# Four pairs by seven products in the down projections and in gate and up, with half tiles and plain banks added by transfers

## The chip, the cores and the metric

The kernel runs on one core of a Trainium2 chip. The metric is the device time of one execution in microseconds (us). A core has five engines that run side by side, each through its own instructions in order: TensorE (PE in the profile; its weight loads are PEld), VectorE (DVE), ScalarE (ACT), GpSimd (POOL) and SyncE (SP). Here SP and POOL only start transfers, apart from a few copies on POOL in the linear attention. TensorE writes its results to eight PSUM banks; VectorE and ScalarE take them out to the on-chip memory, SBUF.

## The reference

One residual block on x (256 frames by 2048), all in float32:

```
x = x + 1/2 * SwiGLU_1(RMSNorm(x))          SwiGLU(h) = (silu(h @ w_gate) * (h @ w_up)) @ w_down
h = RMSNorm(x);  P = h @ W_in               all projections of the mixing part
m = sigmoid(gate_gdn) * (gated_deltanet(P) @ W_A) + sigmoid(gate_att) * (chunk_attention(P) @ W_B)
x = x + m @ W_out
x = x + 1/2 * SwiGLU_2(RMSNorm(x))
```

w_gate and w_up are 2048 by 5504, w_down is 5504 by 2048. The change lies in the two SwiGLU blocks (the FFNs). A k tile below is 128 rows of a weight, of the dimension that is summed over.

## The kernel before, in words

**Products.** For accuracy every float32 operand is split into a high part, rounded to the matmul's format (a ScalarE cast, `L364`, `L395`, `L397`, `L121`), and the rest (a VectorE subtraction, `L418`, `L122`). A product of two blocks is then three matmuls: high by high, high by low, low by high (`product`, L440; `L446` to `L448`). Activations stand still in the array, 128 columns at a time, and weights stream through, 512 columns to a matmul.

**Pairs.** Work goes in pairs: two k tiles, two weights (gate and up, or two column blocks of down) and both halves of the 256 frames. That is a 2 by 2 block product of 8 products, 24 matmuls: a plain pair. Its weights cost one cast and one subtraction of 128x2048. A pair by seven products (Winograd's form of Strassen's method) has 7 products, 21 matmuls. Its weights cost more: VectorE first forms four sums (`L390` to `L392`, tile `s`), then the parts that are used as they are (`w`, `v`) and the sums are split (`L395`, `L397`, three runs of `L418`). Its activations need sums too (`act_sums`, L136).

**seven** (L473) runs eight pairs into PSUM. Plain pairs add into banks 2, 3, 4 and 8, and pairs by seven products into banks 1 to 7. Which pairs go by products is given by a tuple: `FAST` = (0, 2, 5) in gate and up, `DOWN` = (2, 4, 6) in the down of 16 k tiles and in some projections of the mixing part. After the last pair by products, `L513` to `L517` combine banks 1, 5, 6 and 7 into four SBUF tiles (`wide`, eight buffers); after the last pair `L522` adds the four other banks. Four banks (1 to 4) come from the pool `acc`, four from `core`, which transposes use as well.

**An FFN** (`ffn`, L545) has 43 k tiles of hidden width in 11 tiles of gate and up (ten of 4 k tiles, one of 3), in three chunks, `CHUNKS` = tiles 0 to 3, 4 to 7, 8 to 10. After the gate-and-up tiles of a chunk (`gate_up`, L525) comes the chunk's part of the down projection. In the first two chunks it has 16 k tiles and is two runs of `seven`, each for two of the four column blocks. Its four results are added to the residual in DRAM (`xd`) by transfers that add, started on POOL (`L585`). The third chunk's down has 11 k tiles, all plain. It fetches `xd`, adds, and goes on to the norm or the output. The first tile of the first FFN is plain in all pairs, in the order `FIRST`, since the activations still arrive.

**Hidden blocks.** The output of a gate-and-up tile is transposed on TensorE and split (`hidden`, L549) in two jobs, which run in the next tile, late in its pairs (`jobs` in `seven`), or after some steps of the down. For blocks that meet a pair by products in the down, `hidden` also makes and splits sums (`shid`, `hs`).

**Order and memory.** Weights come in one order, given by `plan` (L268). `load` starts the transfers on SP, `begin` (L346) emits the casts and sums of one item, `prepare` (L410) the subtractions; `take_weights` (L423) keeps over five products' or pieces' worth prepared ahead (`PREP`) and two loads beyond that (`LOAD`). A scheduler then puts the instructions of each engine in an order and hands out buffers. Nearly all large tiles share one pool, the heap: `NB` = 23 slots of 128x2048 float32. A plain pair takes three slots (raw, high, low), a pair by products six (raw, s, w, v, sh, sl), although `v` (`w2` in the code, L379) fills only half of its slot. Raw and s come free after the subtractions, the others after the matmuls. Activations of a norm (class `Xr`, L145 on) take a whole slot for a pair by products and half a slot for a plain one: six slots for (0, 2, 5). A down of 16 k tiles holds four slots of hidden blocks and two of their sums besides.

**Mixing** (linear attention, chunk attention, gates, output projection) lies between the FFNs and uses the same heap. Its tile `kd` (L841) fills half a slot.

Of the kernel before, what the change touches and what calls it, by code (L numbers as in the profile page):

```python
# [17 lines left out]
P = 128  # L18
T = 256
D = 2048  # L20
KD = D // P
# [3 lines left out]
W = H * P  # L25
EPS = 1e-6
BIG = 1e30
NB = 23
FAST = (0, 2, 5)
DOWN = (2, 4, 6)  # L30
FIRST = (1, 3, 4, 6, 7, 0, 2, 5)
QUAD = {2: (0, 0), 3: (1, 0), 4: (0, 1), 8: (1, 1)}
CHUNKS = ((0, 4), (4, 8), (8, 11))
B32 = 32
# [4 lines left out]
def block_kernel(ctx: ExitStack, tc: tile.TileContext, a: dict, out: bass.AP):  # L39
# [14 lines left out]

    def heap(shape, dt, name):
        return hp.tile(shape, dt, tag="h", name=name)

    def acc_bank(name):
        return accp.tile([P, 512], F32, tag="acc", name=name)
# [197 lines left out]
    FG = [(c, min(4, KF - c)) for c in range(0, KF, 4)]  # L257

    def fast_pairs(f, i):
        return () if f == "1" and i == 0 else FAST  # L260

    def pairs_of(f, i):
        return FIRST if f == "1" and i == 0 else range(KD // 2)

    def down_pairs(a0, a1):
        return DOWN if sum(FG[a1 - 1]) - FG[a0][0] == 16 else ()

    def plan():  # L268

        for f in "12":  # L270
            for a0, a1 in CHUNKS:
                for i in range(a0, a1):
                    c, m = FG[i]
                    js = pairs_of(f, i)
                    gu = zip(*(t_pieces(a[w + f], c, m, 0, KD, [2 * j for j in js]) for w in ("wg", "wu")))
                    for j, p in zip(js, gu):
                        yield j in fast_pairs(f, i), p
                k0, k1 = FG[a0][0], sum(FG[a1 - 1])
                cols = lambda d: t_pieces(a["wd" + f], 4 * d, 4, k0, k1)
                if down_pairs(a0, a1):  # L280
                    for d in (0, 2):
                        yield from sevens(cols(d), cols(d + 1))
                else:
                    for d in range(4):
                        yield from twos(cols(d))
            if f == "2":
                return
            yield from mixing()
# [2 lines left out]
        for p in pieces:  # L291
            yield False, (p, next(pieces))

    def sevens(one, two):
        for j, pieces in enumerate(zip(one, two)):
            yield j in DOWN, pieces

    def mixing():
        c0 = 0
# [46 lines left out]
    def begin():  # L346


        while len(loaded) < 1 + LOAD and len(loaded) < left[0]:
            load()  # L350
        left[0] -= 1
        i, fast, pieces, raw = loaded.popleft()
        if not fast:
            out = []
            ms = [n * kk * (P if len(src.shape) == 3 else 1) for src, n, kk in pieces]
            cuts = [(slice(0, 2), ms[0])] if ms[0] == ms[1] else [(slice(at, at + 1), m) for at, m in enumerate(ms)]
            hl = [heap([P, 2, 1024], F32R, f"w{x}{i}") for x in "hl"]
            if i < 3:
                cuts = [(slice(at, at + 1), m) for at, m in enumerate(ms)]
            todo = [tuple(w[:, at, :m] for w in (*hl, raw)) for at, m in cuts]  # L360
            if i == 0:
                todo = [tuple(by_k(w[:, at], k) for w in (*hl, raw)) for at in range(2) for k in range(2)]
            for hi, _, src in todo:
                nc.scalar.copy(hi, src)  # L364
            for at, (src, n, kk) in enumerate(pieces):
                if len(src.shape) == 3:
                    n *= P
                    cols = [w[:, at, : ms[at]].rearrange("p (c k x) -> p c k x", k=kk, x=P) for w in hl]
                    cols = [[w[:, :, j, :] for j in range(kk)] for w in cols]
                else:  # L370
                    cols = [[w[:, at, j * n : (j + 1) * n] for j in range(kk)] for w in hl]
                out.append((1, (*cols, n)))
            begun.append((todo, out))
            return
        tiled = len(pieces[0][0].shape) == 3
        n = pieces[0][1] * (P if tiled else 1)
        s = heap([P, 4, n], F32, f"s{i}")
        w1 = heap([P, 2, 2 * n], F32R, f"w{i}")
        w2 = heap([P, 2, n], F32R, f"v{i}")  # L379

        def by_row(w):

            if tiled:
                return w.rearrange("p b (c k x) -> p b k c x", k=2, x=P)
            return w.rearrange("p b (k n) -> p b k n", k=2)

        col = lambda w: w.rearrange("p (c x) -> p c x", x=P) if tiled else w
        R = by_row(raw[:, :, : 2 * n])
        S = s.rearrange("p b (c x) -> p b c x", x=P) if tiled else s
        nc.vector.tensor_sub(S[:, 0:2], R[:, 1], R[:, :, 0])  # L390
        nc.vector.tensor_add(S[:, 2], S[:, 1], R[:, 0, 0])
        nc.vector.tensor_sub(S[:, 3], R[:, 0, 1], S[:, 2])  # L392
        parts = [(w1[:, 0], w1[:, 1], raw[:, 0, : 2 * n]), (col(w2[:, 0]), col(w2[:, 1]), R[:, 1, 1])]
        for hi, lo, src in parts:
            nc.scalar.copy(hi, src)  # L395
        sh, sl = (heap([P, 4, n], F32R, f"s{x}{i}") for x in "hl")
        nc.scalar.copy(sh, s)  # L397
        parts.append((sh, sl, s))
        k = by_row(w1)
        w11, w21 = ([k[:, s, b] for s in range(2)] for b in range(2))  # L400
        t1, t3, t2, t4 = ((sh[:, b], sl[:, b]) for b in range(4))
        w22 = (w2[:, 0], w2[:, 1])

        prods = ((1, 0, w11), (2, 2, w21), (6, 5, t2), (7, 6, t3), (4, 3, t4), (5, 4, t1), (3, 7, w22))
        begun.append((parts, [(4, prods)]))
# [64 lines left out]
        return tp.tile([P, 512], F32, name=name, tag="w", bufs=8)[:, :n]  # L470


    def seven(nm, n, fast, act, jobs=(), feed=None, pairs=range(KD // 2)):  # L473

        size = {b: len(fast) for b in range(1, 9)}
        for b in (2, 3, 4, 8):
            size[b] += 2 * (KD // 2 - len(fast))
        size[8] -= len(fast)  # L480
        done = dict.fromkeys(size, 0)
        banks = {}

        def add(b, act, wt):
            if b not in banks:
                banks[b] = (acc_bank if b < 5 else core_bank)(f"p{nm}_{b}")[:, :n]
            done[b] += 1
            product(banks[b], act, wt, done[b] == 1, done[b] == size[b])

        ev = {}  # L490
        idle = 0
        for at_pair, j in enumerate(pairs):
            if j in fast:
                ps = take_weights()
                for at, (b, i7, w) in enumerate(ps):
                    add(b, act(j, i7), w)
                    if at == 3:
                        tick()
            else:
                for s in range(2):  # L500
                    wh, wl, _ = take_weights()
                    if feed and s == 0:
                        feed(at_pair)
                    for k, w in enumerate(zip(wh, wl)):
                        for t in range(2):
                            add((2, 4, 3, 8)[2 * s + t], act(j, 2 * k + t), w)
                    idle += 1
                    if idle > 3 and jobs and j > max(fast, default=-1):
                        jobs.popleft()()
            if fast and j == fast[-1]:  # L510
                idle = 1
                g0, u0, g1, u1 = (wide(f"e{nm}_{x}", n) for x in range(4))
                nc.scalar.copy(g0, banks[1])  # L513
                nc.vector.tensor_add(u0, banks[6], g0)
                nc.vector.tensor_add(g1, banks[7], u0)
                nc.vector.tensor_add(u1, banks[5], g1)
                nc.vector.tensor_add(u0, banks[5], u0)  # L517
                ev = {2: g0, 3: u0, 4: g1, 8: u1}
        if not fast:
            return banks  # L520
        for b in (2, 3, 4, 8):
            nc.vector.tensor_add(ev[b], banks[b], ev[b])  # L522
        return ev
# [21 lines left out]
    def ffn(nm, xr, nxt, feed):  # L545
# [15 lines left out]
        for a0, a1 in CHUNKS:  # L561
# [18 lines left out]
            if fast:  # L580
                block = lambda j, b: act(2 * j + b // 2, b % 2) if b < 4 else [sums[j][:, s, b - 4] for s in range(2)]
                for d in (0, 2):
                    ev = seven(f"d{nm}_{a0}{d}", 512, fast, block)
                    for b, (dd, t) in QUAD.items():
                        nc.gpsimd.dma_start(xd[d + dd][t], ev[b], accum_op=ALU.add)  # L585
                continue
            for d in range(4):
                pd = pair(f"pd{nm}_{a0}{d}")
# [244 lines left out]
    def gdn_core(blk, dec, res):  # L833
# [4 lines left out]
        yield 1  # L838

        ss = sp.tile([P, 2, 2, H], F32, name="gdn_ss")  # L840
        kd = heap([P, H, P], F32, "gdn_kd")  # L841
        sqb = heap([P, 4, 4, P], F32, "gdn_sq")
        for i, src in enumerate((KT, QT)):
            for t in range(2):
# [246 lines left out]
                yield 1  # L1091


    xr1 = Xr("1", 0, FAST)

    def stand(k4):

# [19 lines left out]
    def feed(s):  # L1117
# [6 lines left out]
            nc.sync.dma_start(cst, a["cst"])  # L1124
        if s == 6:
            nc.sync.dma_start(hd, a["hd"].partition_broadcast(P))
        if s > 1 and FIRST[s] in FAST:
            xr1.more(FIRST[s], pair_of_x(FIRST[s]))
        for k4 in range(4):
            if s == max(3, *(FIRST.index(2 * k4 + i) for i in range(2))):  # L1130
# [71 lines left out]
            nc.vector.tensor_add(G1[t][:, cs], G1[t][:, cs], s)  # L1202
        after(2, lambda d=d: merged(d))

    xr3 = Xr("3", 2, FAST)
    for d in range(4):
        pss = pair(f"pwo{d}")
        xs = fetch(d, "wo")
# [2 lines left out]
            nc.vector.tensor_add(xs[t], xs[t], pss[t])  # L1211
        norm(xr3, d, xs)

    ffn("3", xr3, None, lambda s: s == 4 and xr3.finish())


# [83 lines left out]
```

## Time and profile before

| What | Value |
|---|---|
| Time, median of 3 runs | 2122.12 us (2122.1 to 2122.61) |
| The profiled execution | 2122.12 us |
| its span in the trace | 2120.4 us |
| granted TensorE clock, mean | 0.999 |
| HBM traffic | 407.72 MB read, 16.79 MB written |
| transfers that add to `xd` (POOL) | 32, 256 KB each |

The profile gives for each engine its busy time, the chain of work that ended last, followed back from the end, and groups of equal instructions with their busy time, their mean duration and the idle time of the engine just before them, with what ended most of it. The two FFNs take 0 to 707.8 us and 1424 to 2120.4 us of the span; the mixing lies between. Matmul records overlap, so the pace of TensorE is read from one start to the next, not from the length of a record.

### The profile page before, as it was taken

The numbers are of one execution on the slowest core, as the hardware profiler recorded it, in microseconds if no ns is written. First come the engines' busy times: TensorE is split into PE (matmuls) and PEld (weight loads), VectorE is DVE, ScalarE is ACT, GpSimd is POOL, SyncE is SP. The second block draws the span as 40 slices with busy tenths as digits, with TensorE's granted clock in tenths as the row PEclk, the third lists the DMA queues.
The fourth block names the chain that finished last, engine by engine and source line by source line (L and its number), as shares of the span: only waits on it lengthen the run. The fifth ranks groups of instructions, "written<-read, shape, count | busy, mean of one in ns | idle before, by whom it ended". The sixth has DMA issues, their size and how long they took to land.

```text
span 2120.4 us, 25501 instructions
## 1 busy us (share of the span) xinstructions
PE 2106.7 (99%) x9804; PEld 1755.5 (83%) x9804; DVE 1704.8 (80%) x1867; ACT 1126.7 (53%) x1125; POOL 36.5 (2%) x45
## 2 busy tenths in 40 slices
PE   9999999999999999999999999999999999999999
PEld 6888888888898988888888888888888888888897
DVE  6888898889976688767785787669888997989782
ACT  6655564545555556567555554456454564545461
POOL 0000000000000000000010000000000100000000
PEclk9999999999999999999999999999999999999999
DMA  9655785558867656536454467666565975569582
GB/s 326 198 186 182 230 250 190 190 164 241 245 196 234 236 179 231 166 120 199 144 179 160 139 200 249 217 197 224 189 195 160 258 231 185 179 180 276 174 275 68
DMA packets 393594, 426.19 MB, mean 201 GB/s; under 512 B 14192, under 2 KB 371840, under 8 KB 393216
## 3 DMA queue, kind: packets, MB, share of 16 engines
q1 hardware_dynamic: 388864, 416.17, 60.6%
q0 software_dynamic: 4608, 8.39, 2.4%
q8 instruction: 77, 1.26, 0.3%
q14 instruction: 45, 0.37, 0.1%
HBM read 407.72 MB, written 16.79 MB: 200 GB/s over the span
## 4 chain that ended last, share of the span: by engine, by line
PE 94%; DVE 3%; ACT 1%; issue 1%; DMA 0%; SPq 0%; DVEq 0%; ACTq 0%
PE pf L447 14%; PE pf L448 14%; PE pf L446 13%; PE pd L447 7%; PE pd L448 7%; PE pd L446 7%; PE pg L447 2%; PE pg L448 2%; PE pg L446 2%; PE pc L446 2%; PE pc L448 2%; PE pc L447 2%; PE pwo L447 1%; PE pwo L446 1%; PE pwo L448 1%; PE hid L131 1%
## 5 line engine op out<-in xcount | busy, mean ns | idle before, releaser
L418 DVE TENSOR_TENSOR wl<-raw,wh 128x2048 fp32r<-128x2048 f32 (+5 forms) x302 | 642.6, 2137 | 68.8 <-ACT wh L364 19.6
L364 ACT CAST wh<-raw 128x2048 fp32r<-128x2048 f32 (+5 forms) x302 | 533.9, 1789 | 130.1 <-PE pd L447 27.3
L446 PE MATMUL pf<-wh,xr 128*128 128x512 f32 (+1 forms) x880 | 337.7, 388 | 3.3 <-ACT xr L173 2.4
L447 PE MATMUL pf<-wl,xr 128*128 128x512 f32 (+1 forms) x880 | 339.3, 386 | 0.2 <-DVE wl L418 0.2
L448 PE MATMUL pf<-wh,xr 128*128 128x512 f32 (+1 forms) x880 | 339.0, 385 | 0.0
L397 ACT CAST sh<-s 128x2048 fp32r<-128x2048 f32 (+1 forms) x99 | 187.0, 1889 | 216.0 <-DVE s L392 204.0
L418 DVE TENSOR_TENSOR sl<-s,sh 128x2048 fp32r<-128x2048 f32 (+1 forms) x99 | 223.5, 2258 | 18.8 <-PE pf L448 6.6
L447 PE MATMUL pd<-wl,hid 128*128 128x512 f32 x496 | 195.4, 394 | 0.0
L446 PEld LDWEIGHTS pf<-wh,xr 128*128 128x128 f32 x880 | 165.4, 188 | 36.1 <-ACT xr L173 2.8
L447 PEld LDWEIGHTS pf<-wl,xr 128*128 128x128 f32 x880 | 165.7, 188 | 33.1 <-DVE wl L418 2.1
L448 PE MATMUL pd<-wh,hid 128*128 128x512 f32 x496 | 193.0, 390 | 0.0
L448 PEld LDWEIGHTS pf<-wh,xr 128*128 128x128 f32 x880 | 165.6, 188 | 31.8 <-DVE xr L174 0.4
L446 PE MATMUL pd<-wh,hid 128*128 128x512 f32 x496 | 185.2, 394 | 0.0
L395 ACT CAST w<-raw 128x1024 fp32r<-128x1024 f32 (+1 forms) x99 | 102.9, 1040 | 119.2 <-PE pd L448 31.3
L390 DVE TENSOR_TENSOR s<-raw 128x1024 f32<-128x1024 f32 (+1 forms) x99 | 119.4, 1206 | 23.6 <-PE pd L447 17.6
L418 DVE TENSOR_TENSOR w<-raw,w 128x1024 fp32r<-128x1024 f32 (+1 forms) x99 | 119.5, 1207 | 6.2 <-ACT w L395 6.0
L447 PEld LDWEIGHTS pd<-wl,hid 128*128 128x128 f32 x496 | 93.2, 188 | 23.5 <-DVE wl L418 5.2
L522 DVE TENSOR_TENSOR ef<-pf,ef 128x512 f32<-128x512 f32 (+1 forms) x84 | 55.5, 675 | 69.2 <-PE pf L448 69.2
L446 PEld LDWEIGHTS pd<-wh,hid 128*128 128x128 f32 x496 | 93.1, 188 | 19.7 <-issue 0.7
L448 PEld LDWEIGHTS pd<-wh,hid 128*128 128x128 f32 x496 | 93.1, 188 | 18.9
L446 PE MATMUL pf<-sh,xf 128*128 128x512 f32 (+1 forms) x252 | 95.9, 386 | 1.7 <-ACT sh L397 1.7
L447 PE MATMUL pf<-sl,xf 128*128 128x512 f32 (+1 forms) x252 | 96.7, 384 | 0.0
(472 smaller groups left out, 3837.0 us busy)
## 6 DMA issues: line engine op xcount, KB each, us to landing
raw<-wd SPq DMA_DIRECT2D x168, 512.0 KB, 5.4
raw<-wg SPq DMA_DIRECT2D x159, 512.0 KB, 3.9
raw<-wu SPq DMA_DIRECT2D x159, 512.0 KB, 5.3
raw<-wgt SPq DMA_DIRECT2D x64, 512.0 KB, 4.5
raw<-wa SPq DMA_DIRECT2D x48, 512.0 KB, 4.6
raw<-wc SPq DMA_DIRECT2D x48, 512.0 KB, 4.7
raw<-wbr SPq DMA_DIRECT2D x32, 512.0 KB, 5.4
raw<-wo SPq DMA_DIRECT2D x32, 512.0 KB, 5.1
```

The lines of the kernel that those rows point to most:

```text
L131: nc.tensor.transpose(ps[:, c * T + t * P : c * T + (t + 1) * P], src(t)[:, (c0 + c) * P : (c0 + c + 1) * P], ident)
L364: nc.scalar.copy(hi, src)
L390: nc.vector.tensor_sub(S[:, 0:2], R[:, 1], R[:, :, 0])
L395: nc.scalar.copy(hi, src)
L397: nc.scalar.copy(sh, s)
L418: nc.vector.tensor_sub(lo, src, f32(hi))
L446: nc.tensor.matmul(dst, ah, wh, start=start, stop=False)
L447: nc.tensor.matmul(dst, ah, wl, start=False, stop=False)
L448: nc.tensor.matmul(dst, al, wh, start=False, stop=stop)
L522: nc.vector.tensor_add(ev[b], banks[b], ev[b])
```

## The change

- Gate and up: the first two tiles of each chunk (but not the plain first tile) have four pairs by products, `FOUR` = (0, 2, 4, 6); the other tiles have (0, 2, 4) in place of (0, 2, 5). `FIRST` and the norm's blocks follow.
- The down of 16 k tiles has four pairs by products, `DEEP` = (2, 3, 5, 6), in place of (2, 4, 6).
- In these downs `L522` is not done. The combined tiles go to `xd` by a transfer that adds, each of the four plain banks is copied by ScalarE to another tile, and that goes to `xd` by a second such transfer.
- `w2` and `kd` move to a pool of two half tiles; the heap has 22 slots in place of 23.
- In `seven`, jobs that are left at the last pair all run after its second half. The norm of the second FFN is finished at the fourth pair in place of the fifth.

```diff
-NB = 23
-FAST = (0, 2, 5)
+NB = 22
+NH = 2
+FAST = (0, 2, 4)
+FOUR = (0, 2, 4, 6)
 DOWN = (2, 4, 6)
-FIRST = (1, 3, 4, 6, 7, 0, 2, 5)
+DEEP = (2, 3, 5, 6)
+FIRST = (1, 3, 5, 7, 0, 2, 4, 6)
...
+    def half_tile(shape, dt, name):
+        return hp.tile(shape, dt, tag="q", name=name, bufs=NH)
...
     def fast_pairs(f, i):
-        return () if f == "1" and i == 0 else FAST
+        if f == "1" and i == 0:
+            return ()
+        return FOUR if any(a0 <= i < a0 + 2 for a0, _ in CHUNKS) else FAST
...
     def down_pairs(a0, a1):
-        return DOWN if sum(FG[a1 - 1]) - FG[a0][0] == 16 else ()
+        return DEEP if sum(FG[a1 - 1]) - FG[a0][0] == 16 else ()
...
-                        yield from sevens(cols(d), cols(d + 1))
+                        yield from sevens(cols(d), cols(d + 1), DEEP)
...
-    def sevens(one, two):
+    def sevens(one, two, fast=DOWN):
         for j, pieces in enumerate(zip(one, two)):
-            yield j in DOWN, pieces
+            yield j in fast, pieces
...
-        w2 = heap([P, 2, n], F32R, f"v{i}")
+        w2 = half_tile([P, 2, n], F32R, f"v{i}")
...
-    def seven(nm, n, fast, act, jobs=(), feed=None, pairs=range(KD // 2)):
+    def seven(nm, n, fast, act, jobs=(), feed=None, pairs=range(KD // 2), out=None):
...
                     if idle > 3 and jobs and j > max(fast, default=-1):
                         jobs.popleft()()
+                    while at_pair == KD // 2 - 1 and s == 1 and jobs:
+                        jobs.popleft()()
...
+        if out:
+            for b, put in out.items():
+                put(ev[b])
+                e = wide(f"e{nm}_{b}", n)
+                nc.scalar.copy(e, banks[b])
+                put(e)
+            return None
...
                 for d in (0, 2):
-                    ev = seven(f"d{nm}_{a0}{d}", 512, fast, block)
-                    for b, (dd, t) in QUAD.items():
-                        nc.gpsimd.dma_start(xd[d + dd][t], ev[b], accum_op=ALU.add)
+                    out = {
+                        b: lambda e, dst=xd[d + dd][t]: nc.gpsimd.dma_start(dst, e, accum_op=ALU.add)
+                        for b, (dd, t) in QUAD.items()
+                    }
+                    seven(f"d{nm}_{a0}{d}", 512, fast, block, out=out)
...
-        kd = heap([P, H, P], F32, "gdn_kd")
+        kd = half_tile([P, H, P], F32, "gdn_kd")
...
-    xr1 = Xr("1", 0, FAST)
+    xr1 = Xr("1", 0, FOUR)
...
-        if s > 1 and FIRST[s] in FAST:
+        if s > 1 and FIRST[s] in xr1.fast:
...
-    xr3 = Xr("3", 2, FAST)
+    xr3 = Xr("3", 2, FOUR)
...
-    ffn("3", xr3, None, lambda s: s == 4 and xr3.finish())
+    ffn("3", xr3, None, lambda s: s == 3 and xr3.finish())
```

## The prediction

> **What bounds the kernel now.** I read the page first: its busy times, the chain of waits and the costliest groups.
>
> ```profile
> span 2120.4 us, 25501 instructions
> ...
> PE 2106.7 (99%) x9804; PEld 1755.5 (83%) x9804; DVE 1704.8 (80%) x1867; ACT 1126.7 (53%) x1125; POOL 36.5 (2%) x45
> ...
> PE 94%; DVE 3%; ACT 1%; issue 1%; DMA 0%; SPq 0%; DVEq 0%; ACTq 0%
> ```
>
> TensorE is busy all the time and carries 94% of the chain that ended last. Whether a busy TensorE is also a TensorE at its pace shows in the timeline. I take seven matmuls in a row there and give the first and the last.
>
> ```profile
> 139.26 0.39 PE L448 MATMUL pf<-wh,xr 128*128 128x512 f32 x1
> ...
> 140.62 0.39 PE L448 MATMUL pf<-wh,xr 128*128 128x512 f32 x1
> ```
>
> Six steps in 1.36 us make 0.2267 us from one 512-column matmul to the next; the 0.39 us of a record overlap its neighbours. Next come the windows of one whole chunk of the first FFN: its four gate-and-up tiles, then its down projection of 16 k tiles. The columns are the stretch, its length, and the busy time of each engine with its instructions, then clock, DMA share and GB/s.
>
> ```profile
> core 0: us, PE busy (x) PEld busy (x) DVE busy (x) ACT busy (x) POOL busy (x), PEclk, DMA share, GB/s
> ...
> 273.00:314.50 41.50, 41.50 (x185) 34.35 (x184) 40.99 (x39) 24.11 (x18) 3.45 (x4) 1.00 0.87 254
> 314.50:356.90 42.40, 42.40 (x193) 35.11 (x191) 33.34 (x32) 18.93 (x18) 0.00 (x0) 1.00 0.54 174
> 356.90:399.30 42.40, 42.40 (x194) 35.09 (x192) 36.56 (x37) 21.08 (x18) 0.00 (x0) 1.00 0.61 198
> 399.30:442.70 43.40, 42.98 (x194) 34.98 (x192) 40.81 (x42) 25.63 (x23) 0.00 (x0) 1.00 0.66 207
> 442.70:527.90 85.20, 85.08 (x377) 68.94 (x376) 73.82 (x75) 42.99 (x37) 3.51 (x4) 1.00 0.68 204
> ```
>
> The first tile has 183 matmuls by the code (three pairs of 21, five of 24). 183 x 0.2267 = 41.5 us, the whole window at clock 1.00. So FFN time is the number of matmuls times 0.2267 us, and a matmul less is 0.2267 us less, as long as VectorE keeps the weights coming. VectorE is the next limit: 225.5 of 254.9 us in this chunk, and 40.99 of 41.50 in its first tile.
>
> **TensorE: what is removed.** A pair by products has 21 matmuls, a plain pair 24. Gate and up go from three to four such pairs in the first two tiles of each chunk, except the very first tile, which has none: 5 tiles in the first FFN, 6 in the second. Each 16-tile down has two runs of seven-product form, there are two such downs in each FFN, so 8 runs gain a pair. 19 pairs x 3 = 57 matmuls, all 512 wide; PE should read x9747. 57 x 0.2267 = **12.9 us**. Moving the pair 5 to 4 changes no count.
>
> The Trainium skill, "TensorE: Matmul & The Clock Gate", section "Back-to-back issue gap", gives N/2.4 + 2.5 = 216 ns for a warm isolated gap at N = 512, and about 131 ns as a sustained figure in a stream of loads and matmuls. By the first the saving would be 12.3 us, by the second 7.5 us. The trace shows neither but 227 ns, and that stands.
>
> **VectorE and ScalarE: what a pair costs.** From the groups by line:
>
> ```profile
> L418 DVE TENSOR_TENSOR wl<-raw,wh 128x2048 fp32r<-128x2048 f32 (+5 forms) x302 | 642.6, 2137 | 68.8 <-ACT wh L364 19.6 <-issue 14.4 <-PE pd L448 10.4
> L364 ACT CAST wh<-raw 128x2048 fp32r<-128x2048 f32 (+5 forms) x302 | 533.9, 1789 | 130.1 <-PE pd L447 27.3 <-PE pg L447 21.4 <-issue 12.3
> L418 DVE TENSOR_TENSOR sl<-s,sh 128x2048 fp32r<-128x2048 f32 (+1 forms) x99 | 223.5, 2258 | 18.8 <-PE pf L448 6.6 <-PE pav L447 4.2 <-PE pak L448 3.2
> L397 ACT CAST sh<-s 128x2048 fp32r<-128x2048 f32 (+1 forms) x99 | 187.0, 1889 | 216.0 <-DVE s L392 204.0 <-PE pd L447 7.5 <-DVE gs_u L800 2.6
> L418 DVE TENSOR_TENSOR w<-raw,w 128x1024 fp32r<-128x1024 f32 (+1 forms) x99 | 119.5, 1207 | 6.2 <-ACT w L395 6.0
> L390 DVE TENSOR_TENSOR s<-raw 128x1024 f32<-128x1024 f32 (+1 forms) x99 | 119.4, 1206 | 23.6 <-PE pd L447 17.6 <-PE pg L447 5.2 <-DMA raw<-wd 0.4
> L395 ACT CAST w<-raw 128x1024 fp32r<-128x1024 f32 (+1 forms) x99 | 102.9, 1040 | 119.2 <-PE pd L448 31.3 <-PE pf L448 22.9 <-DVE sl L418 18.6
> L418 DVE TENSOR_TENSOR v<-raw,v 128x512 fp32r<-128x512 f32 (+1 forms) x99 | 67.5, 682 | 4.4 <-ACT v L395 4.4
> L391 DVE TENSOR_TENSOR s<-s,raw 128x512 f32<-128x512 f32 (+1 forms) x99 | 67.4, 681 | 0.8
> L392 DVE TENSOR_TENSOR s<-raw,s 128x512 f32<-128x512 f32 (+1 forms) x99 | 67.4, 680 | 0.3
> L395 ACT CAST v<-raw 128x512 fp32r<-128x512 f32 (+1 forms) x99 | 60.7, 613 | 30.9 <-DVE sl L418 9.8 <-PE pd L447 9.5 <-PE pf L447 6.3
> L522 DVE TENSOR_TENSOR ed<-pd,ed 128x512 f32<-128x512 f32 x32 | 21.3, 688 | 0.0
> ```
>
> A plain pair costs VectorE 2.14 us. A pair by products costs 1.21 + 0.68 + 0.68 + 1.21 + 0.68 + 2.26 = 6.72. The swap adds 4.6 by the means; less 0.08 for each of five more instructions, since back to back they start that much before the last record ends (487.65 + 0.69 against 488.26 in the rows further down), it adds 4.2. ScalarE gains 1.89 + 1.04 + 0.61 - 1.79 = 1.75 us. Each 16-tile chunk gets four swaps (two tiles, two runs of down), so VectorE +16.7 to 18.3. One more hidden pair needs sums:
>
> ```profile
> L122 DVE TENSOR_TENSOR hs<-shid,hs 128x512 fp32r<-128x512 f32 x2 | 1.4, 682 | 0.0
> L138 DVE TENSOR_TENSOR shid<-shid,hid 128x128 f32<-128x128 f32 x2 | 0.6, 282 | 0.3 <-ACT shid L557 0.3
> ```
>
> That is 0.68 + 4 x 0.28 = 1.8. The eight final adds of the downs leave VectorE: 8 x (0.69 - 0.08) = 4.9 less. Sum for the chunk: 225.5 + 16.7 + 1.8 - 4.9 = 239.1, up to 240.7 by the larger swap, against TensorE's 254.9 - 12 x 0.2267 = 252.2. VectorE goes from 88 to 95%: full, but not over. First two tiles alone: 40.99 + 33.34 + 8.4 to 9.2, less 2.4 for the four adds of the down before that fall into the first, is 80.3 to 81.1 against 83.9 - 1.4 = 82.5. So gate and up should keep its share of the gain; the cover for VectorE's extra work is 1.5 us there, and if it is gone the tiles last as long as VectorE's work.
>
> **Where weights come late.** In the down, slots of the heap, not VectorE, set when work starts. These rows are from one pair by products, VectorE first, then TensorE's first use of its last tile.
>
> ```profile
> 487.65 0.69 DVE L418 TENSOR_TENSOR v<-raw,v 128x512 fp32r<-128x512 f32 x1
> 488.26 0.69 DVE L522 TENSOR_TENSOR ed<-pd,ed 128x512 f32<-128x512 f32 x1
> ...
> 493.63 2.29 DVE L418 TENSOR_TENSOR sl<-s,sh 128x2048 fp32r<-128x2048 f32 x1 [0.69 <-PE pd L448]
> ```
> ```profile
> 498.81 0.39 PE L447 MATMUL pd<-sl,hs 128*128 128x512 f32 x1
> ```
>
> VectorE waited for a TensorE release and was done at 495.92, 2.9 us ahead of use. Half tiles make a pair by products hold five slots and a half tile in place of six, and the heap has 22 in place of 23: with two such pairs in flight that is the same memory. The new order 2, 3, 5, 6 puts two side by side. Then the second one's slots come free one seven-product pair ahead (21 x 0.2267 = 4.76 us) in place of one plain pair (24 x 0.2267 = 5.44), and the lead falls from 2.9 to about 2.2 us. One VectorE subtraction in the way (2.29) uses that up. There are 16 such second halves. The nearest row of such a wait:
>
> ```profile
> L446 PE MATMUL pd<-sh,hs 128*128 128x512 f32 x72 | 25.3, 397 | 0.5
> L446 PE MATMUL pf<-sh,xf 128*128 128x512 f32 (+1 forms) x252 | 95.9, 386 | 1.7 <-ACT sh L397 1.7
> ```
>
> 0.5 us over the four downs is 0.125 each. I charge 16 x 0.125 = **2.0 us**. Bounds: the 2.2 us of these two rows go too (a gain), or each double costs VectorE's full excess (second rival).
>
> **Banks and transfers.** The last adds of a down become ScalarE copies and a second added transfer each.
>
> ```profile
> L513 ACT COPY ef<-pf 128x512 f32<-128x512 f32 (+1 forms) x21 | 12.1, 575 | 43.8 <-PE pf L448 43.8
> ...
> xd<-ed POOLq DMA_DIRECT2D x32, 256.0 KB, 8.2
> ...
> q0 software_dynamic: 4608, 8.39, 2.4%
> ```
>
> 32 copies of 0.58 us go to an engine busy 43 of 85 us in the down, so banks come free about as early as by the adds. I take nothing; if every copy queued behind one 1.89 us cast, two of a run's four would be late, at most 8 x 1.9 = 15 us, a size that rival 2 covers. 32 transfers more at 2.4% x 2120 / 32 = 1.6 us of all DMA engines put 6.4 us more on a run of 41 us whose DMA share is 0.68, so 0.83. Queued behind a waiting second transfer on POOL are only other added transfers. Nobody reads those blocks until the third chunk's down, three tiles later; the next run or tile takes the buffers again after its sixth pair or later, some 30 us on, which covers two landings (2 x 8.2 us). Cost 0.
>
> Edits with one answer, zero: the new order of the first tile (it is plain before and after), one more block of sums there and after the output projection (2 x 0.68 + 4 x 0.28 = 2.5 us of VectorE each, off TensorE's path unless it comes ahead of a weight: 0 to 2.5 us, I take 0), the norm's end one pair earlier, the key tile of the linear attention in a half tile. Hidden transposes of the second tile now come together after the last pair and need two banks; the combinations then end inside that pair as they do in the down now. The mixing part, in the row below, has one slot less for plain weights beside an idle VectorE (186 us): bound -1 to +2 us, I take 0.
>
> ```profile
> 707.80:1424.00 716.20, 713.82 (x3501) 603.90 (x3500) 529.78 (x692) 396.72 (x441) 8.28 (x9) 1.00 0.57 186
> ```
>
> **Sum.** The profiled execution took 2122.12 us, 1.7 beyond its span, and equals the median of the three runs. 2122.12 - 12.9 + 2.0 = **2111.2 us**.
>
> **Rivals.** (1) Gate and up gain nothing: VectorE at 80.3 to 81.1 of 82.5 us idles now and then for TensorE's last bank, and what it misses TensorE waits for. 11 x 0.68 = 7.5 us are lost: 2118.7. For it: 40.99 of 41.50 us in the first tile already. Against: the second tile has 9 us idle. (2) Slower: the two neighbours in the down. They cost VectorE 2 x 6.3 = 12.5 us while TensorE needs 2 x 4.76 = 9.5, so 3.0 us must be prepared ahead, and the lead seen is 2.9. If slots keep half of that lead back, 16 x 1.5 = 24 us: 2133. It decides the sign from 12.9 / 16 = 0.8 us each. For it: releasers named PE pd. Against: two plain pairs ahead of the first double give VectorE 6.5 us. (3) Products are left in the old number: the counts in the code exclude that.
>
> **How the numbers follow.** Forecast 0.62 (2107.5 to 2115.5), rival 1 0.22 (2115.5 to 2122), rival 2 0.14, better than 2107.5 0.02. About 0.2%, 4.2 us, can be told from no change. Faster by that is below 2117.9: 0.62 + 0.02 + 0.08 of rival 1 = 0.72. Within: 0.14 of rival 1 and 0.03 of rival 2 = 0.17. Slower: 0.11. Range 2107.5 to 2121: the low end is the bare 2109.2 with no new wait less the 1.7 us of old ones; the high end is rival 1 with the 2 us of the mixing's bound.
>
> **What would show it.** PE x9747, wl x283, sl x118, ed adds on L522 gone, POOL transfers x64. Right: down windows of about 83.8 us, first tiles of about 40.8, VectorE 95% in the chunk. Wrong: PE idle before sh or sl in the down over 5 us, a first or second tile as long as before with VectorE at 99%, or a mixing part longer than 718 us.

## The result, and the profile after

The changed kernel takes 2108.12 us (median of four runs, 2107.68 to 2108.96). The kernel before took 2122.22 us beside it (four runs, 2122.1 to 2122.61). The ratio is 0.9934, with a 95% interval of 0.9917 to 0.9951: 14.1 us less, where 10.9 were forecast. The execution that was profiled took 2107.68 us.

From the page of the kernel after come the span, the busy times, the chain that ended last, and the queue of the adding transfers with the time from their issue to their landing:

```profile
span 2105.9 us, 25649 instructions
...
PE 2090.3 (99%) x9747; PEld 1746.8 (83%) x9747; DVE 1767.7 (84%) x1959; ACT 1179.4 (56%) x1208; POOL 64.5 (3%) x77
...
q0 software_dynamic: 9216, 16.78, 4.5%
...
PE 96%; DVE 2%; SPq 1%; issue 0%; DMA 0%; ACT 0%; DVEq 0%; ACTq 0%
...
xd<-ed POOLq DMA_DIRECT2D x64, 256.0 KB, 6.9
```

TensorE has the 9747 matmuls of the count and is still the bound. VectorE's share rose from 80 to 84%, but its part in the chain fell from 3 to 2%. Next come the windows of the same chunk of the first FFN (four tiles, then the down), and of the mixing, with the columns of the prediction's table:

```profile
265.90:311.40 45.50, 45.50 (x202) 37.48 (x202) 45.25 (x42) 28.51 (x25) 5.26 (x6) 1.00 0.95 271
311.40:353.00 41.60, 41.60 (x190) 34.53 (x188) 40.92 (x39) 23.31 (x21) 0.00 (x0) 1.00 0.62 203
353.00:395.60 42.60, 42.60 (x195) 35.24 (x193) 40.23 (x48) 24.49 (x25) 0.00 (x0) 1.00 0.54 173
395.60:438.00 42.40, 42.40 (x193) 35.10 (x191) 37.95 (x36) 22.51 (x21) 0.00 (x0) 1.00 0.62 199
438.00:517.70 79.70, 78.77 (x349) 64.24 (x348) 73.55 (x75) 45.41 (x43) 8.69 (x10) 1.00 0.78 228
700.80:1417.00 716.20, 713.82 (x3501) 603.99 (x3500) 529.12 (x692) 397.38 (x441) 8.27 (x9) 1.00 0.57 186
```

The edges of the first and the fifth stretch lie elsewhere than before: TensorE starts the next stage's first pair before the last one ends (202 records in the tile, 349 in the down). So read the sum. The chunk went from 254.9 to 251.8 us, with VectorE busy for 237.9 of them, 94.5%. The fourth tile lost 1.0 us although no matmul was removed there. The mixing takes 716.20 us, as before.

What TensorE waited for shows in the list of what its weight loads waited for (us in total, times, longest), first before, then after:

```profile
PEld pd L447 <- DVE wl L418: 5.2, 20, 0.3
PEld pf L446 <- ACT sh L397: 3.4, 4, 0.8
...
PEld pd L446 <- ACT sh L397: 2.2, 4, 0.5
PEld pf L447 <- DVE wl L418: 2.1, 5, 0.5
```
```profile
PEld pd L454 <- ACT sh L405: 5.4, 4, 1.4
PEld pd L455 <- DVE sl L426: 2.5, 8, 0.3
...
PEld pf L454 <- ACT sh L405: 1.2, 5, 0.2
...
PEld pf L455 <- DVE wl L426: 0.4, 1, 0.4
```

The four rows come to 12.9 us before and to 9.5 after. A weight load runs ahead of its matmul, so TensorE itself waits less: for `sh` in the down, after, the loads waited 5.4 us and TensorE 3.7. The groups give the idle time of TensorE itself (in the last column), and the new copies:

```profile
L454 PE MATMUL pf<-sh,xf 128*128 128x512 f32 (+1 forms) x296 | 112.0, 386 | 0.0
L454 PE MATMUL pd<-sh,hs 128*128 128x512 f32 x96 | 35.9, 394 | 3.7 <-ACT sh L405 3.7
L533 ACT COPY ed<-pd 128x512 f32<-128x512 f32 x32 | 17.6, 591 | 7.8 <-PE pd L456 7.8
```

The wait for `sh` in gate and up went from 1.7 to 0.0 us, the one in the down rose from 0.5 to 3.7. The waits moved and changed in size, so the two halves of the change were run apart.

### The profile page after: what moved, and what is told of

Read it like the earlier page. It is cut to its first block, busy times and chain, and to the rows that moved or that the text cites. A ratio compares the mean times of both kernels' runs of the same rounds, so it can differ in the third digit from the quotient of the medians.

```text
span 2105.9 us, 25649 instructions
## 1 busy us (share of the span) xinstructions
PE 2090.3 (99%) x9747; PEld 1746.8 (83%) x9747; DVE 1767.7 (84%) x1959; ACT 1179.4 (56%) x1208; POOL 64.5 (3%) x77
## 4 chain that ended last, share of the span: by engine, by line
PE 96%; DVE 2%; SPq 1%; issue 0%; DMA 0%; ACT 0%; DVEq 0%; ACTq 0%
PE pf L454 14%; PE pf L456 14%; PE pf L455 14%; PE pd L455 7%; PE pd L456 7%; PE pd L454 7%; PE pg L455 2%; PE pg L456 2%; PE pg L454 2%; PE pc L454 2%; PE pc L456 2%; PE pc L455 2%; PE pwo L456 1%; PE pwo L454 1%; PE pwo L455 1%; DVE wl L426 1%
## 5 line engine op out<-in xcount | busy, mean ns | idle before, releaser
L426 DVE TENSOR_TENSOR wl<-raw,wh 128x2048 fp32r<-128x2048 f32 (+5 forms) x283 | 598.7, 2125 | 70.5 <-PE pc L455 16.9
L426 DVE TENSOR_TENSOR sl<-s,sh 128x2048 fp32r<-128x2048 f32 (+1 forms) x118 | 265.8, 2258 | 26.8 <-PE pd L455 11.9
L455 PE MATMUL pf<-wl,xr 128*128 128x512 f32 (+1 forms) x704 | 271.4, 386 | 0.0
L456 PE MATMUL pf<-wh,xr 128*128 128x512 f32 (+1 forms) x704 | 271.3, 385 | 0.0
L454 PE MATMUL pf<-wh,xr 128*128 128x512 f32 (+1 forms) x704 | 262.2, 387 | 2.2 <-ACT xr L179 1.5
L456 PE MATMUL pd<-wh,hid 128*128 128x512 f32 x432 | 169.1, 391 | 0.0
L454 PE MATMUL pd<-wh,hid 128*128 128x512 f32 x432 | 163.6, 392 | 0.0
L454 PEld LDWEIGHTS pf<-wh,xr 128*128 128x128 f32 x704 | 132.7, 189 | 28.3 <-ACT xr L179 1.9
L456 PEld LDWEIGHTS pf<-wh,xr 128*128 128x128 f32 x704 | 132.5, 188 | 25.4 <-DVE xr L180 0.2
L403 ACT CAST v<-raw 128x512 fp32r<-128x512 f32 (+1 forms) x118 | 72.6, 615 | 91.3 <-PE pf L456 30.9
L456 PE MATMUL pf<-sh,xf 128*128 128x512 f32 (+1 forms) x296 | 113.5, 385 | 0.0
L454 PE MATMUL pf<-sh,xf 128*128 128x512 f32 (+1 forms) x296 | 112.0, 386 | 0.0
L601 POOL DMA_DIRECT2D xd<-ed x64 | 56.0, 997 | 1305.7 <-ACT ed L523 1228.1
L456 PEld LDWEIGHTS pd<-wh,hid 128*128 128x128 f32 x432 | 81.1, 188 | 17.2
```

Of the source, the lines that this page charges most:

```text
L426: nc.vector.tensor_sub(lo, src, f32(hi))
L454: nc.tensor.matmul(dst, ah, wh, start=start, stop=False)
L455: nc.tensor.matmul(dst, ah, wl, start=False, stop=False)
L456: nc.tensor.matmul(dst, al, wh, start=False, stop=stop)
L601: b: lambda e, dst=xd[d + dd][t]: nc.gpsimd.dma_start(dst, e, accum_op=ALU.add)
```

## The experiments

The theory at the start: the gain is the 57 matmuls at 0.227 us (12.9 us), and the rest comes from waits that went. The rivals: gate and up gain nothing, because VectorE is full; or the neighbours in the down cost much and something else pays for them. Below, "less" and "more" are differences to the kernel before, measured beside each version, by medians.

**Gate and up alone.** The down is as before, its last adds and single transfers too (their diff is that of the third experiment).

```diff
-DEEP = (2, 3, 5, 6)
+DEEP = (2, 4, 6)
```


> The change without its down part: four pairs by products in the first two tiles of each chunk, half tiles, 22 slots, but the down with pairs 2, 4, 6 and its last adds on VectorE. Count theory (each matmul removed is 0.227 us, VectorE keeps up): 33 matmuls are 7.5 us, and if the new order and the half tiles also take away the waits of sh at the fourth tiles of the 16-tile chunks (3.4 us in gaps of 0.58 and 0.28 us between matmul starts, before), 2111 to 2115. Rival (gate and up gain nothing, because VectorE is full in the first two tiles): 2118 to 2122.

Measured: 2112.83 us, 9.5 less, ratio 0.9954 (0.9939 to 0.9969). That is inside the first range. The count gives 33 x 0.2267 = 7.5, so this half gained more than its count. A full VectorE did not take the gain.

**The down alone.** Gate and up have three pairs in the old order.

```diff
-FAST = (0, 2, 4)
-FOUR = (0, 2, 4, 6)
+FAST = (0, 2, 5)
+FOUR = (0, 2, 5)
...
-FIRST = (1, 3, 5, 7, 0, 2, 4, 6)
+FIRST = (1, 3, 4, 6, 7, 0, 2, 5)
...
-    ffn("3", xr3, None, lambda s: s == 3 and xr3.finish())
+    ffn("3", xr3, None, lambda s: s == 4 and xr3.finish())
```


> The change without its gate-and-up part: pairs 0, 2, 5 in all tiles as before, but the down with 2, 3, 5, 6, ScalarE copies, added transfers, half tiles. Count theory: 24 matmuls are 5.4 us; the changed kernel's gap of 1.1 us in each of the four downs costs 4.4, where the old kernel had 0.28: 2118 to 2121 if the waits at the fourth tiles stay, 2116 to 2118 if the half tiles take them away. Rival (two neighbours cost VectorE's excess): above 2122.

Measured: 2117.33 us, 5.0 less, ratio 0.9977 (0.9967 to 0.9986), where the count gives 24 x 0.2267 = 5.4. The two halves together make 14.5, about the whole, and by these medians what the count doesn't explain lies in gate and up. The split is not a clean one: both halves hold the half tiles, and the ten runs of this one spread from 2114.84 to 2120.37. The time is that of the second range, but not for its reason. In the profiled execution, the slowest of the ten, TensorE still waits for `sh` in gate and up (2.6 us, 4 times), while the 3.7 us for `sh` in the down are not in its list; 2.6 us for `wl` in the down (2 times) are. So the waits of one half depend on the other.

**Final adds on VectorE, one transfer each.**

```diff
-                    seven(f"d{nm}_{a0}{d}", 512, fast, block, out=out)
+                    ev = seven(f"d{nm}_{a0}{d}", 512, fast, block)
+                    for b, (dd, t) in QUAD.items():
+                        nc.gpsimd.dma_start(xd[d + dd][t], ev[b], accum_op=ALU.add)
```


> The changed kernel with the last adds of the down on VectorE again and one transfer for each result. Count theory: VectorE goes from 239 to about 244 of 252 us in a chunk, still under TensorE; within 1.5 us of the changed kernel (2107 to 2110). Rival: VectorE is the limit at the seam between a down and the next tile, where it is 99% busy: 2.4 us in each of eight runs is late, 2112 to 2127.

Measured: 2111.24 us, 11.1 less, ratio 0.9947 (0.9931 to 0.9964); its four runs (2110.07 to 2111.55) are all above those of the kernel after. So by the medians the copies and second transfers cost nothing and give some 3 us, between the two expectations; the intervals of the two ratios overlap. The waits of the weight loads show a part of it: at the seam from the down to the next tile adds stand between the steps of the sums, and the loads of `sh` in gate and up wait for 4.4 us in all where it was 1.2.

```profile
PEld pf L454 <- ACT sh L405: 4.4, 9, 0.6
```

**The pairs of the down apart from each other.** No neighbours any more; the same count.

```diff
-DEEP = (2, 3, 5, 6)
+DEEP = (0, 2, 4, 6)
```


> The changed kernel with pairs 0, 2, 4, 6 in the down, so that no two by products are neighbours. The count of matmuls is the same. If the new wait of 1.1 us in each down comes from the neighbours 2 and 3, it goes: 2103 to 2105. If it comes from VectorE's load or from slots as such, it stays or moves: 2107 to 2112, and 2112 or more if the two plain pairs at the head of a run were what let VectorE get ahead.

Measured: 2122.96 us, 0.6 more, ratio 1.0006 (0.9996 to 1.0015): no gain is left, 14.7 us against the kernel after for the same matmuls. What TensorE itself waited for in this kernel (us in total, times, longest):

```profile
PE pd L454 <- ACT sh L405: 6.9, 16, 0.9
PE pf L454 <- ACT sh L405: 4.9, 2, 2.5
```

So taking the neighbours apart doesn't help, and waits of 0.9 us stand in each down without them too. But this edit does two things. In the downs TensorE now waits for `sh` 16 times (0.43 us on average; the downs have 32 pairs by products). And pair 0 needs sums of hidden blocks of a chunk's first tile, which had none, so the work of other engines is put in another order. The two waits of 2.5 us stand some 19 us into a third tile of gate and up, at its last pair by products. VectorE had done `s` there at 117.99, but ScalarE's cast of `sh` stood behind a copy out of a bank that waited for TensorE:

```profile
119.57 0.59 ACT L523 COPY ef<-pf 128x512 f32<-128x512 f32 x1 [8.12 <-PE pf L456]
```

The cast started at 120.05, 2.06 us after `s` was done. So these two waits come from ScalarE's order, not from VectorE's load. How the 14.7 us split stays open: the waits shown are 11.8 us, against 3.7.

**Four pairs in all tiles.** A pair more in ten tiles (the expectation counted nine); the page has 9717 matmuls, 30 fewer than after.

```diff
-        return FOUR if any(a0 <= i < a0 + 2 for a0, _ in CHUNKS) else FAST
+        return FOUR
```


> The changed kernel with four pairs by products in all tiles of gate and up but the first: nine tiles more, 27 matmuls or about 6 us less (8 of them 512 wide, one 384 wide). Count theory without a limit of VectorE: 2102 to 2103. Theory that VectorE is the next limit: two more swaps of 4.2 us put it from 239 to about 247 of 250.8 us in a chunk, so TensorE waits: 2108 or more, and TensorE idle behind sh or sl in the third and fourth tiles.

Measured: 2119.17 us, 2.9 less, ratio 0.9987 (0.9977 to 0.9996), so 11 us worse than after with fewer matmuls. The groups:

```profile
L455 PE MATMUL pd<-wl,hid 128*128 128x512 f32 x432 | 170.3, 394 | 3.5 <-DVE wl L426 3.5
L454 PE MATMUL pf<-sh,xf 128*128 128x512 f32 (+1 forms) x336 | 124.7, 387 | 7.6 <-ACT sh L405 7.6
```

The windows over the same chunk sum to 253.4 us, with VectorE busy for 245.37, or 96.8%:

```profile
sum 253.40, PE 250.35 PEld 205.28 DVE 245.37 ACT 146.87 POOL 13.97; mean PE 50.07 PEld 41.06 DVE 49.07 ACT 29.37 POOL 2.79
```

TensorE now waits for `sh` and `wl`, as the second theory had it. At four of the six waits for `sh` in gate and up the cast starts as soon as VectorE is done with `s`, and VectorE had not paused in the 9 us before: there it no longer follows, which is the first rival one step further on. The other two (1.9 us together) are of another kind. `s` was done 2.0 us before the cast, which stood behind ScalarE's cast of `v`; that one waited for TensorE's last matmul with an earlier `v`, and there are two half tiles for `v`. The edit also puts the last pair by products of the third and fourth tiles at place 6 in place of 4, so that their hidden blocks are split later. How much of the 11 us is a full VectorE and how much the order, this run does not separate.

**Whole slots for the half tiles.**

```diff
-NB = 22
+NB = 23
...
-        w2 = half_tile([P, 2, n], F32R, f"v{i}")
+        w2 = heap([P, 2, n], F32R, f"v{i}")
...
-        kd = half_tile([P, H, P], F32, "gdn_kd")
+        kd = heap([P, H, P], F32, "gdn_kd")
```


> The changed kernel without half tiles: 23 slots, and a pair by products takes six again (the same memory). If slots limit how early weights are prepared in the down, the neighbours 2 and 3, 5 and 6 are late: 16 places by 0.5 to 1.5 us, 2116 to 2132. If the half tiles matter little: 2107 to 2110.

Measured: 2111.26 us, 10.8 less, ratio 0.995 (0.9933 to 0.9966): by the medians the half tiles are worth about 3 us in the whole change, less than the first expectation and more than the second; the interval overlaps with that of the kernel after. The weight loads of the down waited here for `sh`, `sl` and `wl` for 6.0, 4.5 and 3.5 us, against 5.4, 2.5 and none after.

**Half tiles alone**, in the kernel before.

```diff
-NB = 23
+NB = 22
...
+    def half_tile(shape, dt, name):
+        return hp.tile(shape, dt, tag="q", name=name, bufs=2)
...
-        w2 = heap([P, 2, n], F32R, f"v{i}")
+        w2 = half_tile([P, 2, n], F32R, f"v{i}")
...
-        kd = heap([P, H, P], F32, "gdn_kd")
+        kd = half_tile([P, H, P], F32, "gdn_kd")
```


> The kernel before with half tiles and 22 slots and nothing else. No matmul less. If the slots that this frees took away the waits of sh at the fourth tiles: 2118 to 2120; if not, 2121 to 2124, the upper part if 22 slots hold up the plain stretches.

Measured: 2124.22 us, 2.2 more, ratio 1.0011 (1.0002 to 1.0021). In its groups TensorE waits for the last adds out of the banks, which come late:

```profile
L449 PE MATMUL pd<-wh,hid 128*128 128x512 f32 x496 | 189.5, 394 | 2.7 <-DVE ed L525 2.7
```

So the half tiles cost alone and pay beside the rest of the change; which part of it they serve was not run.

**The order alone**, in the kernel before: the last pair by products in gate and up comes one pair earlier. Not one matmul less.

```diff
-FAST = (0, 2, 5)
+FAST = (0, 2, 4)
...
-FIRST = (1, 3, 4, 6, 7, 0, 2, 5)
+FIRST = (1, 3, 5, 6, 7, 0, 2, 4)
...
-    ffn("3", xr3, None, lambda s: s == 4 and xr3.finish())
+    ffn("3", xr3, None, lambda s: s == 3 and xr3.finish())
```


> The kernel before with pairs 0, 2, 4 in place of 0, 2, 5 and nothing else but the orders that follow from it. No matmul less. If the place of the third pair is what took away the waits of sh at the fourth tiles (3.4 us in gaps before, none after): 2118 to 2120. If the half tiles or the rest did that: 2121 to 2123.

Measured: 2118.29 us, 3.7 less, ratio 0.9983 (0.9973 to 0.9992). The wait for `sh` in gate and up is gone from the groups:

```profile
L446 PE MATMUL pf<-sh,xf 128*128 128x512 f32 (+1 forms) x252 | 95.6, 384 | 0.0
```

Why it was there shows in the timeline of the kernel before at the start of the fourth tile (start, length): VectorE, then ScalarE's cast of `sh`, then TensorE.

```profile
400.22 1.22 DVE L390 TENSOR_TENSOR s<-raw 128x1024 f32<-128x1024 f32 x1
401.35 0.69 DVE L122 TENSOR_TENSOR hs<-shid,hs 128x512 fp32r<-128x512 f32 x1
401.95 0.69 DVE L391 TENSOR_TENSOR s<-s,raw 128x512 f32<-128x512 f32 x1
402.55 0.69 DVE L122 TENSOR_TENSOR hid<-hid,hid 128x512 fp32r<-128x512 f32 x1
403.15 0.69 DVE L392 TENSOR_TENSOR s<-raw,s 128x512 f32<-128x512 f32 x1
```
```profile
403.88 1.91 ACT L397 CAST sh<-s 128x2048 fp32r<-128x2048 f32 x1 [1.76 <-DVE s L392]
```
```profile
405.84 0.96 PE L446 MATMUL pf<-sh,xf 128*128 128x512 f32 x3 [0.42 <-ACT sh L397]
```

The splits of the hidden blocks (`hs`, `hid`) stand between the three steps of `s`; the cast waits 1.76 us, TensorE 0.42. `seven` runs these jobs only after several halves of plain pairs behind the last pair by products. With that pair at place 4 they run a pair earlier, ahead of the seam. That 0.42 us is not all that is lost there: the matmul before starts at 405.03, so this one starts 405.84 - 405.03 - 0.23 = 0.58 us late. Both kernels have 9804 matmuls, so the starts of their traces can be laid beside each other. The order gains 0.9 to 1.0 us in the fourth tile of each of the four chunks of 16 k tiles, and loses 1.0 us in the very first tile, whose order it changes too.

**Four neighbours in the down.**

```diff
-DEEP = (2, 3, 5, 6)
+DEEP = (3, 4, 5, 6)
```


> The changed kernel with pairs 3, 4, 5, 6 in the down: four by products in a row behind three plain ones, same count of matmuls. If neighbours cost VectorE's excess beyond a lead of about 3 us: a row needs 4 x 6.3 = 25 us of VectorE in 19 us of TensorE, so 3 us or more are missing in each of eight runs, 2125 to 2135. If only VectorE's total in a run counts, it is the same: 2107 to 2110.

Measured: 2116.56 us, 5.7 less, ratio 0.9974 (0.9964 to 0.9984): 8.4 us worse than after, about 1 us for each of the 8 runs. Neither theory had that. A row of neighbours thus costs less than the second rival made it, even if all of the 8.4 us is its price. In the list of what TensorE waited for, 1.9 us stand for `sl` in the down, 3.2 us for the copies out of the banks (`ed`, L533) and 3.1 us for `sh` in gate and up; only the first is a wait for the weights of the row. The hidden sums move with this edit too, and the runs don't separate the two.

**One apart, three in a row.**

```diff
-DEEP = (2, 3, 5, 6)
+DEEP = (2, 4, 5, 6)
```


> The changed kernel with pairs 2, 4, 5, 6 in the down: one alone, then three in a row. Neighbour theory: three need 18.8 us of VectorE in 14.3, 4.5 us ahead, about 1.5 us more than the lead, in eight runs: 2114 to 2122. If the gap of 1.1 us in the first run of each down comes from pair 3 standing next to pair 2 while the hidden blocks are split, that gap goes and the gain offsets part: 2108 to 2114.

Measured: 2121.04 us, 1.3 less, ratio 0.9994 (0.9985 to 1.0003), 12.9 us worse than after, and inside the range of the neighbour theory. TensorE's weight loads wait for VectorE in the down, 16 times:

```profile
PEld pd L455 <- DVE wl L426: 11.3, 16, 2.1
```

TensorE itself waited for 5.7 us of that, and for 1.6 us for `sl` in the down. But 3.9 us are for `sh` in gate and up, where nothing was edited, so the neighbours' price is not shown alone here either.

**The first run of each down with three pairs.** The four waits of 5.4 us in the kernel after are one in each down, in its first run. Here is one, in the timeline of the kernel after, VectorE, then ScalarE, then TensorE:

```profile
451.40 2.29 DVE L426 TENSOR_TENSOR sl<-s,sh 128x2048 fp32r<-128x2048 f32 x1 [1.21 <-PE pd L456]
453.61 0.28 DVE L144 TENSOR_TENSOR shid<-shid,hid 128x128 f32<-128x128 f32 x1
...
455.39 0.69 DVE L128 TENSOR_TENSOR hs<-shid,hs 128x512 fp32r<-128x512 f32 x1
455.99 1.22 DVE L398 TENSOR_TENSOR s<-raw 128x1024 f32<-128x1024 f32 x1
...
458.98 0.69 DVE L400 TENSOR_TENSOR s<-raw,s 128x512 f32<-128x512 f32 x1
```
```profile
459.60 0.63 ACT L403 CAST v<-raw 128x512 fp32r<-128x512 f32 x1 [2.81 <-PE pd L456]
460.12 1.90 ACT L405 CAST sh<-s 128x2048 fp32r<-128x2048 f32 x1
```
```profile
460.76 0.39 PE L456 MATMUL pd<-w,hid 128*128 128x512 f32 x1
462.08 0.74 PE L454 MATMUL pd<-sh,hs 128*128 128x512 f32 x2 [0.93 <-ACT sh L405]
```

The sums of the last hidden blocks come just when the neighbours 2 and 3 have used up the lead; `s` is done at 459.67 and TensorE starts 462.08 - 460.76 - 0.23 = 1.1 us late. The late matmul is not pair 3's, though: all 42 matmuls of the pairs 2 and 3 start from 449.84 to 459.17 without a wait. It is one of pair 5, the first five of which stand in TensorE's order behind the first four of the plain pair 4. Of the 1.1 us, 0.45 are not VectorE's: the cast of `sh` starts only at 460.12, behind that of a `v` which is needed later, for which ScalarE stood idle until TensorE's last matmul with an earlier `v` was done (459.17 + 0.39 = 459.56): there are two half tiles, and both were in use. The other three waits show the same 0.45. In the second run there are no hidden sums, and no wait. So the first run gets one pair by products fewer, 12 matmuls more in the kernel:

```diff
+RUN = {0: (2, 5, 6), 2: DEEP}
...
-                        yield from sevens(cols(d), cols(d + 1), DEEP)
+                        yield from sevens(cols(d), cols(d + 1), RUN[d])
...
-                    seven(f"d{nm}_{a0}{d}", 512, fast, block, out=out)
+                    seven(f"d{nm}_{a0}{d}", 512, RUN[d], block, out=out)
```


> The changed kernel with pairs 2, 5, 6 by products in the first of the two runs of a down, and 2, 3, 5, 6 in the second. 12 matmuls more, 2.7 us. If the gap of 1.1 us comes from the first run's neighbours 2 and 3 falling together with the hidden blocks' sums, 4.4 us go: 2106 to 2107. If it comes from elsewhere (the next pair, the slots): 2110 to 2111.

Measured: 2105.94 us, 16.4 less, ratio 0.9927 (0.9913 to 0.994). The groups (lines one further down):

```profile
L455 PE MATMUL pd<-sh,hs 128*128 128x512 f32 x84 | 30.7, 389 | 0.0
```

The wait is gone, and the kernel is about 2 us ahead of the kernel after by the medians, with 12 matmuls more. The intervals of the two ratios overlap. The edit takes away the weight sums and the half tile of pair 3 together, and in this kernel no matmul of pair 5 stands in pair 4 any more, so it doesn't say how much of the wait was due to each.

**The last tile with four pairs too**, on top of that.

```diff
-        return FOUR if any(a0 <= i < a0 + 2 for a0, _ in CHUNKS) else FAST
+        return FOUR if i == len(FG) - 1 or any(a0 <= i < a0 + 2 for a0, _ in CHUNKS) else FAST
```


> The kernel with pairs 2, 5, 6 in the first run of a down, and four pairs by products also in the eleventh tile of gate and up of both FFNs (384 columns wide). 6 matmuls of 384 columns less, 0.173 us each: 1.0 us. If VectorE's limit is one of the place (the down that follows this tile is all plain and leaves VectorE 40 to 55% idle), they come off in full: 2104 to 2106, no new wait of TensorE. If VectorE is full everywhere in gate and up, as in the run with four pairs in all tiles: 2107 to 2110.

Measured: 2105.58 us, 16.6 less, ratio 0.9925 (0.9911 to 0.9939). The span of the profiled execution is 0.9 us shorter than that of the run before it; the time lies in the first range, but by the times the two can't be told apart. It is the fastest version here by its median.

## Why the prediction was right, and where it was off

- **The count and its price: right.** 57 matmuls went, PE reads x9747. The chunk took 251.8 us where the sum had 252.2, and the two halves gave 9.5 and 5.0 us against counts of 7.5 and 5.4.
- **VectorE full, but not over: right.** 237.9 us in the chunk, where 239.1 to 240.7 were worked out, and 94.5% against 95. With four pairs in all tiles most of the gain went, in part because VectorE no longer followed.
- **Windows of single stages: could not be read as announced.** Down windows of 83.8 us and first tiles of 40.8 were to show it. The first tile has 45.5 and the down 79.7, only because the stages now overlap at their seam; their sum, 125.2, stands against 124.6. Read alone, a first tile longer than before with VectorE busy for 45.25 of 45.50 us is the sign of being wrong that the prediction named; its 202 records show that a part of the down lies in it.
- **The waits: the term that was mis-sized.** The prediction put "16 x 0.125 = 2.0 us" on the sum, said "Moving the pair 5 to 4 changes no count", and listed the new order among the "edits with one answer, zero". The count indeed stays. But the order alone is worth 3.7 us (0.9983, 0.9973 to 0.9992), because it moves the splits of hidden blocks away from the sums that the next tile's first weights need. The new wait in the down doesn't come at the second of two neighbours, where it was argued, but at the matmuls of pair 5 that stand in pair 4, in 4 places, not 16, and at some 0.9 us each: 3.7 us in the row, 3.2 more than before. A wait of VectorE for TensorE, of the kind that the prediction named, stands ahead of it (1.21 us at 451.40), but so do two things that it did not weigh there: the hidden sums, and a cast that is held up by the half tiles. The gain was 3.2 us larger than forecast (14.1 against 10.9): 2.0 is the charge that wasn't due on balance, and 1.2 is a net gain (14.1 - 12.9). That the time still lies inside the range, 0.6 us above its low end, owes something to luck: what the order gained and what the new waits cost nearly cancelled. By the pieces: -3.7 for the order and +3.2 for the new waits leave -0.7 for others. The small waits for `wl` in the down, 20 of up to 0.3 us before, are no longer in the list; that they are the rest was not tested alone.
- **Banks and transfers at zero: not worse, but better.** A copy took 0.59 us (0.58 taken), the transfers landed in 6.9 us (8.2 before) with all engines taken 4.5% of the time, and the down's DMA share was 0.78 (0.83 forecast). By the medians the kernel is 3 us slower with the adds on VectorE: taken off a full engine, the adds were worth something that the sum held only as VectorE time.
- **The mixing at zero: right,** 716.20 us both times.
- **First rival (gate and up gain nothing): refuted** by gate and up alone. With four pairs everywhere it holds in part.
- **Second rival (the neighbours cost too much): refuted for this change,** which is faster and not slower, and a down without neighbours gained nothing. Its arithmetic, VectorE slower than TensorE over a row of pairs by products, fits the time of one apart and three in a row (2121.04, inside 2114 to 2122), but four in a row cost less (8.4 us, of which 1.9 stand as waits for the row's weights). Why alternation is worst was not settled: where hidden sums fall, and what stands ahead of a cast on ScalarE, changes with every such edit.

## What to carry to other kernels

When a change trades work of the bound engine for work of the next one, work out the second engine's share stage by stage: here the whole count was earned at 94.5%, and at 96.8%, with 30 matmuls fewer and another order of the jobs, the kernel was 11 us slower. With so little slack the order is worth as much as the count, since the same 57 matmuls saved gave between 14.1 us and nothing, depending only on which pairs of the down carry them; so look for every other job, on the second engine and on the one that feeds it, that falls between a weight's load and its use, and run an edit of the order alone as an experiment of its own. Memory edits that cost alone (half tiles, 2.2 us) can pay beside the change that they serve (3 us), so judge them together.

## What the runs showed of the hardware that was not expected

In the kernel with the down's pairs apart, TensorE ran at half its clock after a wait of 2.47 us. The timeline of TensorE around one of its two long waits:

```profile
119.14 0.39 PE L456 MATMUL pf<-w,xf 128*128 128x512 f32 x1
122.00 0.73 PE L454 MATMUL pf<-sh,xf 128*128 128x512 f32 x2 [2.47 <-ACT sh L405]
...
123.56 0.63 PE L456 MATMUL pf<-wh,xr 128*128 128x512 f32 x1
123.98 0.63 PE L454 MATMUL pf<-wh,xr 128*128 128x512 f32 x1
...
126.45 0.39 PE L455 MATMUL pf<-wl,xr 128*128 128x512 f32 x1
```

The windows over the wait, the start after it, and the stretch behind, with the granted clock third from the end:

```profile
119.50:122.00 2.50, 0.03 (x1) 0.00 (x0) 0.71 (x2) 2.43 (x3) 0.00 (x0) 1.00 1.07 360
122.00:122.90 0.90, 0.90 (x4) 0.76 (x5) 0.90 (x1) 0.90 (x1) 0.00 (x0) 1.00 1.06 349
123.10:126.20 3.10, 3.10 (x9) 2.42 (x8) 3.10 (x2) 3.10 (x3) 0.00 (x0) 0.50 0.56 190
126.50:129.00 2.50, 2.50 (x13) 2.02 (x12) 2.29 (x1) 1.38 (x2) 0.00 (x0) 1.00 0.00 0
```

The clock stays full for about a microsecond after the wait and is then 0.50 for some 3.4 us, with 0.43 us from matmul to matmul in place of 0.227. Seven or eight matmuls lose 0.2 us each, about 1.5 us on top of the 2.47. The Trainium skill, "TensorE: Matmul & The Clock Gate", section "HAM oscillation — how this bites in real kernels", states the rule as no idle gaps of TensorE above about 3.4 us. This trace doesn't agree: 2.47 us were enough. The length of the wait alone doesn't decide it. In the kernel before, a wait of 2.40 us at 21.3 us was followed by a clock of 0.50 (23.0 to 25.5 us); in the kernel with three pairs in the first run of each down, a wait of 2.42 us at the same place was not (1.00 from 21.3 to 27.0 us).
